# Weight-sum steps moved ahead of an output projection, and the third and fifth activation forms reordered in an MLP's down stages

## The chip, the cores and the metric

The kernel runs on one core of one Trainium2 chip. The metric is the device time of one execution in microseconds, lower is better. The kernel before took 833.65 us (median of 3 runs, 831.7 to 833.7).

## The reference

One encoder layer on 512 tokens of width 1024, in float32: a token mixer (two recurrent head groups behind one input projection, then an output projection), a cross attention on 256 memory tokens, and an MLP of width 4096.

```python
x = x + token_mixer(rmsnorm(x, norm_mix[l]), w_in[l], ...)
x = x + cross_attention(rmsnorm(x, norm_xattn[l]), rmsnorm(mem, norm_mem[l]), w_xq[l], w_xkv[l], w_xo[l])
x = x + squared_relu_mlp(rmsnorm(x, norm_mlp[l]), w_up[l], w_down[l])
return rmsnorm(x, norm_final)

def squared_relu_mlp(xn, w_up, w_down):
    return jnp.square(jax.nn.relu(xn @ w_up)) @ w_down
```

## The kernel before

Every float32 operand is split into a high and a low float32r half (`split_out`, L347: ScalarE writes the high half, VectorE subtracts and writes the low half). A product then is three matmuls: high by high, high by low, low by high. Two splits of a weight tile of 128x1024 feed 12 or 24 matmuls.

From the output projection of the cross attention on, products go by blocks of 2x2 with seven products, P1 to P7, in place of eight. Each product multiplies a **form** of the activations (a block, or a sum of blocks) by a form of the weights. Each of them comes in two halves, 0 and 1, so a stage has 14 jobs; "(P5, 1)" is product P5 with half 1, and in the code's order strings "5b" is the same. The MLP has eight stages: 0, 2, 4 and 6 multiply by `w_up` (function `up`, L1547), 1, 3, 5 and 7 by `w_down` (function `by_blocks`, L1296). The output projection is `by_blocks` with stage -1; the text calls it the output projection, and the odd MLP stages the down stages.

**Weight sums.** The sums of weight blocks for the MLP are made in HBM while the earlier parts of the kernel run. `make_forms` (L309) lists the steps: a copy of a block or of an earlier sum, issued on SyncE's queue (L305 and L321, tile `form_P`), or a transfer that adds a block onto the sum, issued on GpSimd's queue (L305, `form_P<-in_wpk`). `allow(n)` (L250) hands out credit: a copy costs 1, an addition 2. It is called once for each weight tile of the projections (`weights`, L289) and, in the output projection, once for each job with `allow(2)` (L1320). An addition is ordered after the newest weight split on VectorE (`last_made`). SyncE's queue also carries the loads of the weight tiles (tile `st`, L269 and L305), three buffers deep. The sums of the output projection itself are made in SBUF by additions on GpSimd's queue (`add_block`, L1185, tiles `gate` and `as`): after P7's weights are split, another block is added onto the same tile `gate` for P6, and after P6's once more for P4.

**Orders.** TensorE's order is that in which the code is written. VectorE, ScalarE, GpSimd and SyncE are ordered by a scheduler, with `tc.high_priority()` lifting what it encloses; `behind(a, b)` puts instruction a behind b on its engine.

**Forms of the MLP's activations.** An `up` stage makes the forms for the down stage after it: `first(g)` makes P5's, `second` P6's, `by_p3` P3's, `by_p7` P7's, and an unnamed block under `if p in ("P3", "P6")` makes P2's. Some of them are put off into the down stage by the table `turn`, each ahead of a given job. A down stage adds its products onto the residual, tiles `vv`, by `add_to` (L1522, eviction L1525).

Of the kernel before, what the change touches and what calls it, by code (L numbers as in the profile page):

```python
# [80 lines left out]
def trunk(ctx: ExitStack, tc: tile.TileContext, x, mem, wpk, vec, cst, lmask, rmask, rows, out):  # L81
# [201 lines left out]
    def weights(key):  # L283
        i = SIDX[key]
        with (tc.high_priority() if i > 2 else ExitStack()):
            for n in range(i, i + 3):
                split(n)
            load(i + 3)
        allow(0 if i < 6 else 1 if key[1] == "kv" else 2)  # L289
        return hl_tiles[i]  # L290

    mforms = {}
# [930 lines left out]
        MORDER += [seq("1a 5a 1b 6a 2a 3a 7a 5b 6b 4a 2b 7b 3b 4b" if q else "1a 1b 2a 2b 5a 5b 6a 6b 7a 7b 4a 3a 4b 3b"),  # L1223
                   two(*("P1", "P5", "P6", "P2", "P7", "P3", "P4") if q < 3 else ("P1", "P5", "P2", "P6", "P3", "P7", "P4"))]
    MJ = [(st, p, g) for st in range(8) for p, g in MORDER[st]]
    mst, mhl, msum = {}, {}, []

    def mload(n):
        if n < len(MJ) and n not in mst:
# [27 lines left out]
    def msplit(n):  # L1257
        if n >= len(MJ):
            return
        if n not in mhl:  # L1260
            for w in [w for w in due if w[0] <= n]:
                due.remove(w)
                w[1](*w[2:])
            st, p, g = MJ[n]
            mload(n)
            hi, lo = T("wh", 1024, 3, F32R), T("wl", 1024, 3, F32R)
            made = split_out(hi, lo, mst[n])
            last_made[0] = made[1]
            if n == 1:
                q_made[0] = made  # L1270
            mhl[n] = (hi, lo)
            if st % 2 and p == "P6":
                due.append((n + 1, sum_add, st, "P4", g))
            if st % 2 and p in ("P5", "P4") and st < 7:
                q = {"P5": "P5", "P4": "P6"}[p]
                due.append((n + 3, sum_base, st + 2, q, g))
                due.append((n + 7, sum_add, st + 2, q, g))
        return mhl[n]
# [17 lines left out]
    def by_blocks(st, sta, banks, done, ready=None, after=None):  # L1296

        mlp = st >= 0
        user = {"P1": 0, "P2": 1, "P5": 2, "P6": 0, "P3": 2, "P7": 0 if mlp else 3, "P4": 0}
        opens = {"P1", "P2", "P5"} if mlp else {"P1", "P2", "P5", "P7"}  # L1300
        jobs = MORDER[st] if mlp else JOBS
        held = {}

        def product(p, g, u, w, first, end):
            for k in range(2):
                ah, al = [t[:, u * P:u * P + P] for t in sta[2 * g + k][p]]
                bh, bl = [t[:, k * 512:k * 512 + 512] for t in w]
                new = first and k == 0 and p in opens
                fl = dict(skip_group_check=True)
                ps = held[user[p]][u]  # L1310
                pe.matmul(ps, lhsT=ah, rhs=bh, start=new, stop=False, **fl)  # L1311
                pe.matmul(ps, lhsT=ah, rhs=bl, start=False, stop=False, **fl)  # L1312
                pe.matmul(ps, lhsT=al, rhs=bh, start=False, stop=end and k == 1, **fl)  # L1313
            if after is not None:
                after()

        def ahead(n):
            if mlp:
                return mahead(len(JOBS) * st + n)
            allow(2)  # L1320
            with tc.high_priority():
                for m in range(n, n + 3):
                    job(m)
                i = max(hl_tiles)
                for m in range(i + 1, i + 4):
                    load(m)
                for m in range(n + 3 - len(JOBS), n + 7 - len(JOBS)):
                    if m >= 0:
                        mload(m)
            return job(n)  # L1330

        def finished(p, u):
            for t0, c, sign in INTO[mlp][p]:
                done(t0 + u, c, held[user[p]][u], sign, (p, t0, c) in LAST[mlp])

        n = 0
        while n < len(jobs):
            p, g = jobs[n]
            if ready is not None:
                ready(p, g)  # L1340
            if user[p] not in held:
                held[user[p]] = banks[user[p]]()
            if p == "P4":
                ws = [ahead(n), ahead(n + 1)]
                for u in range(2):
                    for g in range(2):
                        product(p, g, u, ws[g], False, g == 1)
                    finished(p, u)
                n += 2
                continue  # L1350
            w = ahead(n)
            for u in range(2):
                product(p, g, u, w, g == 0, g == 1)
                if g == 1:
                    finished(p, u)
            n += 1
# [165 lines left out]
    def add_to(t, c, ps, sign, fin=False):  # L1522
        z = xr[t, c]
        with tc.high_priority():
            added = v.tensor_tensor(out=z, in0=z, in1=ps, op=ALU.add if sign > 0 else ALU.subtract)  # L1525
        if not fin:
            return
        squared = stats(st3, t, c)
# [18 lines left out]
    def up(st):  # L1547
# [4 lines left out]
        def square(t, src):  # L1552
            sc.activation(t, src, AF.Relu)
            sc.activation(t, t, AF.Square)

        def form(p, g, src, buf):
            t = buf(F32R)
            split_out(t[:, 0:512], t[:, 512:1024], src)
            forms[p, g] = t

        def first(g):
            v.tensor_tensor(out=y[3, g], in0=y[2, g], in1=y[3, g], op=ALU.subtract)
            form("P5", g, y[3, g], A4)

        def second(g):
            v.tensor_tensor(out=y[3, g], in0=y[3, g], in1=y[0, g], op=ALU.subtract)
# [8 lines left out]
            form("P7", g, y[0, g], A4)  # L1575

        yt = lambda dt: YT1(dt)
        done = set()
        for n, (p, g) in enumerate(MORDER[st]):
            hi, lo = mahead(len(JOBS) * st + n)  # L1580
            if p == "P1":
# [30 lines left out]
            elif p == "P6":  # L1612
                y[1, g] = rrow[:, (1 - g) * 512:(1 - g) * 512 + 512]
                with tc.high_priority():
                    sc.activation(y[1, g], ps, AF.Copy)
            if p in ("P3", "P6") and {("P3", g), ("P6", g)} <= set(MORDER[st][:n + 1]):
                z = y[1, g]
                v.tensor_tensor(out=z, in0=C[g], in1=z, op=ALU.subtract)
                square(z, z)
                form("P2", g, z, G4)  # L1620
                done.add(("P2", g))
                if ("P4", 0) in done and g == 0:
                    by_p3(0)
            if p == "P7":
                with tc.high_priority():
                    v.tensor_tensor(out=y[3, g], in0=y[3, g], in1=ps, op=ALU.subtract)
# [2 lines left out]
            elif p == "P4":  # L1629
                y[2, g] = T2()[:, 0:512]  # L1630
                with tc.high_priority():
                    square(y[2, g], ps)
                    first(g)
                done.add(("P4", g))
                if g == 0:
                    second(g)
                    by_p7(g)
                    if ("P2", 0) in done:
                        by_p3(g)
        sta = [{} for _ in range(4)]  # L1640

        def hand(g):
# [3 lines left out]
                        sta[2 * g + k][p] = t[:, k * 256:k * 256 + 256], t[:, 512 + k * 256:768 + k * 256]  # L1646

        def ready(p, g):
            for at, fn in turn:
                if (p, g) == at:  # L1650
                    with (tc.high_priority() if fn is second else ExitStack()):
                        fn(1)
                    hand(1)

        turn = ((("P1", 1), second), (("P6", 0), by_p7), (("P2", 0), by_p3))
        if st == 6:
            turn = ((("P1", 1), second), (("P2", 0), by_p3), (("P6", 0), by_p7))
        hand(0)
        hand(1)
        return sta, ready  # L1660
# [97 lines left out]
```

## Time and profile before

| | us |
|---|---|
| median of 3 runs | 833.65 |
| profiled execution, its own time | 833.5 |
| its span, first to last instruction | 831.7 |
| around the span | 1.8 |

The span runs from the mixer's input projection (0 to about 300) over the cross attention (to 447), its output projection (447 to 499) and the MLP's eight stages (499 to the end). In a row of the timeline the columns are start, duration, engine, line, operation, output and input tiles, and in brackets the idle time before it with what ended it. PE is TensorE's matmuls, DVE VectorE, ACT ScalarE, POOL GpSimd. A matmul's duration overlaps the next one, so TensorE's pace is read from the distance of starts. A row of the waits has the waiting engine and line, whom it waited for, the total, the number of times and the longest.

### The profile page before, as it was taken

The numbers are of one execution on the slowest core, as the hardware profiler recorded it, in microseconds if no ns is written. First come the engines' busy times: TensorE is split into PE (matmuls) and PEld (weight loads), VectorE is DVE, ScalarE is ACT, GpSimd is POOL, SyncE is SP. The second block draws the span as 40 slices with busy tenths as digits, with TensorE's granted clock in tenths as the row PEclk, the third lists the DMA queues.
The fourth block names the chain that finished last, engine by engine and source line by source line (L and its number), as shares of the span: only waits on it lengthen the run. The fifth ranks groups of instructions, "written<-read, shape, count | busy, mean of one in ns | idle before, by whom it ended". The sixth has DMA issues, their size and how long they took to land.

```text
span 831.7 us, 14078 instructions
## 1 busy us (share of the span) xinstructions
PE 808.2 (97%) x5438; PEld 696.1 (84%) x5438; DVE 619.1 (74%) x1033; ACT 485.7 (58%) x854; POOL 95.4 (11%) x130
## 2 busy tenths in 40 slices
PE   9999999999999999999999989989999999999995
PEld 6787878877889988887888869978998899789984
DVE  6568885699479898546568859997479658875995
ACT  5247464545577585345455658863586458546854
POOL 2000111201121110211122201010001000100001
PEclk9999999999999999999999999999999999999998
DMA  7367677765795787895689985686866796768552
GB/s 275 117 244 258 149 165 174 206 219 135 182 281 133 185 238 261 249 243 134 148 256 196 237 192 179 203 206 197 261 196 152 227 279 190 171 207 268 178 152 102
DMA packets 56597, 167.26 MB, mean 201 GB/s; under 512 B 5393, under 2 KB 5521, under 8 KB 56530
## 3 DMA queue, kind: packets, MB, share of 16 engines
q1 hardware_dynamic: 41200, 126.04, 44.2%
q0 software_dynamic: 15040, 39.85, 26.4%
q8 instruction: 43, 0.70, 0.3%
q10 hardware_dynamic: 290, 0.47, 0.2%
q14 instruction: 24, 0.20, 0.1%
HBM read 164.24 MB, written 48.23 MB: 255 GB/s over the span
## 4 chain that ended last, share of the span: by engine, by line
PE 77%; DVE 11%; DMA 5%; issue 3%; ACT 2%; POOL 1%; POOLq 0%; SPq 0%; DVEq 0%; ACTq 0%
PE mm L351 11%; PE mm L353 11%; PE mm L352 11%; PE sm L1313 4%; PE sm L1596 4%; PE sm L1311 4%; PE sm L1597 4%; PE sm L1312 4%; PE sm L1595 4%; DVE wl L348 3%; PE mm L1596 3%; PE mm L1597 3%; PE mm L1595 3%; DMA form_P<-form_P 2%; DMA gate<-in_wpk 2%
## 5 line engine op out<-in xcount | busy, mean ns | idle before, releaser
L348 DVE TENSOR_TENSOR wl<-st,wh 128x1024 fp32r<-128x1024 f32 x165 | 201.5, 1223 | 103.2 <-ACT wh L348 102.2
L348 ACT ACTIVATE wh<-st 128x1024 fp32r<-128x1024 f32 x165 | 174.1, 1057 | 167.0 <-PE mm L352 43.9
L351 PE MATMUL mm<-xT,wh 128*128 128x512 f32 x288 | 115.5, 402 | 0.0
L353 PE MATMUL mm<-xT,wl 128*128 128x512 f32 x288 | 113.1, 393 | 0.1
L352 PE MATMUL mm<-xT,wh 128*128 128x512 f32 x288 | 112.8, 392 | 0.3 <-DVE xT L1066 0.3
L305 POOL DMA_DIRECT2D form_P<-in_wpk x44 | 44.8, 1028 | 294.2 <-DVE wl L348 228.9
L1311 PE MATMUL sm<-wh,a 128*128 128x512 f32 x180 | 70.8, 394 | 2.4 <-ACT a L348 2.2
L1313 PE MATMUL sm<-wh,a 128*128 128x512 f32 x180 | 71.3, 396 | 1.6 <-DVE a L348 1.5
L1312 PE MATMUL sm<-wl,a 128*128 128x512 f32 x180 | 70.7, 393 | 0.0
L353 PEld LDWEIGHTS mm<-xT,wl 128*128 128x128 f32 x288 | 54.1, 188 | 11.8 <-DVE wl L348 0.3
L352 PEld LDWEIGHTS mm<-xT,wh 128*128 128x128 f32 x288 | 54.2, 188 | 10.9 <-DVE xT L1066 0.9
L351 PEld LDWEIGHTS mm<-xT,wh 128*128 128x128 f32 x288 | 54.2, 188 | 10.8 <-ACT wh L348 0.3
L305 POOL DMA_DIRECT2D as<-in_wpk x20 | 17.5, 911 | 277.5 <-DVE wl L348 171.9
L1313 PEld LDWEIGHTS sm<-wh,a 128*128 128x128 f32 x180 | 34.2, 190 | 10.4 <-DVE a L348 3.4
L1311 PEld LDWEIGHTS sm<-wh,a 128*128 128x128 f32 x180 | 34.2, 190 | 10.2 <-ACT a L348 2.6
L1312 PEld LDWEIGHTS sm<-wl,a 128*128 128x128 f32 x180 | 34.1, 189 | 7.2
L1596 PE MATMUL sm<-yT,wh 128*128 128x256 f32 x128 | 36.3, 284 | 0.7 <-DVE yT L348 0.7
L348 ACT ACTIVATE wh<-as 128x1024 fp32r<-128x1024 f32 x24 | 25.4, 1057 | 19.8 <-PE sm L1313 12.0
L1596 PE MATMUL mm<-xT,wh 128*128 128x256 f32 x128 | 36.3, 284 | 0.2 <-DVE xT L348 0.2
L1596 PE MATMUL sm<-xT,wh 128*128 128x256 f32 x128 | 36.3, 284 | 0.2 <-DVE xT L348 0.2
L1595 PE MATMUL sm<-xT,wh 128*128 128x256 f32 x128 | 36.4, 284 | 0.0
L1595 PE MATMUL mm<-xT,wh 128*128 128x256 f32 x128 | 36.3, 284 | 0.0
(388 smaller groups left out, 2127.8 us busy)
## 6 DMA issues: line engine op xcount, KB each, us to landing
st<-in_wpk SPq DMA_DIRECT2D x123, 512.0 KB, 4.2
form_P<-in_wpk POOLq DMA_DIRECT2D x44, 512.0 KB, 8.3
st<-form_P SPq DMA_DIRECT2D x42, 512.0 KB, 4.4
form_P<-in_wpk SPq DMA_DIRECT2D x26, 512.0 KB, 6.3
as<-in_wpk POOLq DMA_DIRECT2D x24, 512.0 KB, 7.6
form_P<-form_P SPq DMA_DIRECT2D x18, 512.0 KB, 8.6
gate<-in_wpk POOLq DMA_DIRECT2D x8, 512.0 KB, 7.9
as<-form_P SPq DMA_DIRECT2D x8, 512.0 KB, 5.8
```

What stands on the lines that cost most here:

```text
L305: return eng.dma_start(out=dst, in_=mblock(st, g, *b), max_dma_last_dim=4096, **kw)
L348: return sc.activation(dst_hi, src, AF.Copy), v.tensor_tensor(out=dst_lo, in0=src, in1=dst_hi.bitcast(F32), op=ALU.subtract)
L351: pe.matmul(ps, lhsT=ah, rhs=bh, start=first, stop=False)
L352: pe.matmul(ps, lhsT=ah, rhs=bl, start=False, stop=False)
L353: pe.matmul(ps, lhsT=al, rhs=bh, start=False, stop=last)
L1311: pe.matmul(ps, lhsT=ah, rhs=bh, start=new, stop=False, **fl)
L1312: pe.matmul(ps, lhsT=ah, rhs=bl, start=False, stop=False, **fl)
L1313: pe.matmul(ps, lhsT=al, rhs=bh, start=False, stop=end and k == 1, **fl)
L1595: pe.matmul(o, lhsT=hi[:, z], rhs=xh[:, m], start=new, stop=False, **fl)
L1596: pe.matmul(o, lhsT=hi[:, z], rhs=xl[:, m], start=False, stop=False, **fl)
L1597: pe.matmul(o, lhsT=lo[:, z], rhs=xh[:, m], start=False, stop=kt == 3, **fl)
```

## The change

It has three parts. First, the output projection's `allow(2)` is gone, and each weight tile of the input projection (index 6 to 36) hands out 2.5 credits in place of 2; tiles of the key and value projection keep 1, all others 2. Second, the third form of half 0, `by_p3(0)`, always goes into the down stage, ahead of (P5, 1); and the second form of half 1, now `by_p5(1)`, is made after P4's square in stages 2, 4 and 6. Third, two orders are added: the weight split for (P5, 0) of a down stage stands behind the split of the activation form (P5, 1) on both engines, and every eviction of a down stage stands behind that form's low half on VectorE.

```diff
-        allow(0 if i < 6 else 1 if key[1] == "kv" else 2)
+        allow(0 if i < 6 else 1 if key[1] == "kv" else 2.5 if i < 45 else 2)
...
+            if st % 2 and (p, g) == ("P5", 0):
+                for a, b in zip(made, early["P5", 1]):
+                    behind(a, b)
...
         def ahead(n):
             if mlp:
                 return mahead(len(JOBS) * st + n)
-            allow(2)
...
             added = v.tensor_tensor(out=z, in0=z, in1=ps, op=ALU.add if sign > 0 else ALU.subtract)
+        behind(added, early["P5", 1][1])
...
-            split_out(t[:, 0:512], t[:, 512:1024], src)
+            early[p, g] = split_out(t[:, 0:512], t[:, 512:1024], src)
...
+        def by_p5(g):
+            z = y[1, g]
+            v.tensor_tensor(out=z, in0=C[g], in1=z, op=ALU.subtract)
+            square(z, z)
+            form("P2", g, z, G4)
...
-            if p in ("P3", "P6") and {("P3", g), ("P6", g)} <= set(MORDER[st][:n + 1]):
-                z = y[1, g]
-                v.tensor_tensor(out=z, in0=C[g], in1=z, op=ALU.subtract)
-                square(z, z)
-                form("P2", g, z, G4)
-                done.add(("P2", g))
-                if ("P4", 0) in done and g == 0:
-                    by_p3(0)
+            if p in ("P3", "P6") and {("P3", g), ("P6", g)} <= set(MORDER[st][:n + 1]) and (st == 0 or g == 0):
+                by_p5(g)
...
                     second(g)
                     by_p7(g)
-                    if ("P2", 0) in done:
-                        by_p3(g)
+                elif st:
+                    by_p5(g)
...
-        turn = ((("P1", 1), second), (("P6", 0), by_p7), (("P2", 0), by_p3))
+        turn = ((("P1", 1), second, 1), (("P5", 1), by_p3, 0), (("P6", 0), by_p7, 1), (("P2", 0), by_p3, 1))
         if st == 6:
-            turn = ((("P1", 1), second), (("P2", 0), by_p3), (("P6", 0), by_p7))
+            turn = ((("P1", 1), second, 1), (("P5", 1), by_p3, 0), (("P2", 0), by_p3, 1), (("P6", 0), by_p7, 1))
```

TensorE's order is the same in both kernels, and so are ScalarE's and VectorE's up to the end of stage 0. Line numbers of the changed kernel are higher: an eviction is L1527, `first` L1565, `by_p5` L1570, `second` L1575, `by_p3` L1579, `by_p7` L1583.

The first place is GpSimd's queue in the output projection. Before, the additions onto the MLP's sums (`form_P`) stand between and behind the additions onto the projection's own sums (`gate`); the first two rows are the additions for P6, the second pair of `gate` those for P4.

```order
L1187 DMA gate_4301<-in_wpk 128x1024
L1187 DMA gate_4302<-in_wpk 128x1024
L305 DMA form_P_1_3379<-in_wpk 256x1x512
L305 DMA form_P_1_3391<-in_wpk 256x1x512
L305 DMA form_P_0_3376<-in_wpk 256x1x512
L305 DMA form_P_0_3388<-in_wpk 256x1x512
L1187 DMA gate_4301<-in_wpk 128x1024
L1187 DMA gate_4302<-in_wpk 128x1024
L305 DMA form_P_1_3380<-in_wpk 256x1x512
L305 DMA form_P_1_3392<-in_wpk 256x1x512
```

After, nothing stands between the four, and three additions onto MLP sums remain, behind the two small powers of the norm.

```order
L1187 DMA gate_4311<-in_wpk 128x1024
L1187 DMA gate_4312<-in_wpk 128x1024
L1187 DMA gate_4311<-in_wpk 128x1024
L1187 DMA gate_4312<-in_wpk 128x1024
L1448 TENSOR_TENSOR tiny_5047<-tiny_5044,misc 128x2
L1448 TENSOR_TENSOR tiny_5132<-tiny_5129,misc 128x2
L305 DMA form_P_0_2624<-in_wpk 256x1x512
L305 DMA form_P_1_2616<-in_wpk 256x1x512
L305 DMA form_P_1_2628<-in_wpk 256x1x512
```

Six additions, and the copies between them on SyncE's queue, have moved ahead of the projection.

The second place is ScalarE at the end of stage 0 and the start of stage 1. Before, a_853 is the high half of the activation form (P5, 1), a_849 that of (P3, 0), wh_5670 and wh_5692 are the weights of (P5, 0) and (P5, 1), wh_5714 and wh_5734 those of P6.

```order
L348 ACTIVATE wh_5670<-st_5518 128x1024
L348 ACTIVATE a_844_5556<-as_5137 128x512
L348 ACTIVATE wh_5692<-st_5563 128x1024
L1553 ACTIVATE rg_4656<-rg_4656 128x512
L1554 ACTIVATE rg_4656<-rg_4656 128x512
L348 ACTIVATE wh_5714<-as_5138 128x1024
L348 ACTIVATE gate_5665<-rg_4656 128x512
L348 ACTIVATE wh_5734<-as_5138 128x1024
L348 ACTIVATE a_849_5596<-rg_4656 128x512
L348 ACTIVATE a_853_5631<-t_823_5378 128x512
```

After, a_852 is (P5, 1), a_861 is (P6, 1), and wh_5666 and wh_5688 are the weights of P5.

```order
L348 ACTIVATE gate_5592<-rg_4667 128x512
L348 ACTIVATE a_844_5556<-as_5134 128x512
L348 ACTIVATE a_852_5627<-t_823_5378 128x512
L348 ACTIVATE wh_5666<-st_5518 128x1024
L348 ACTIVATE wh_5688<-st_5563 128x1024
L1556 ACTIVATE rg_4667<-rg_4667 128x512
L348 ACTIVATE a_861_5685<-t_823_5378 128x512
```

The form (P5, 1) has moved from behind eight instructions to ahead of P5's own weights, which it now pushes back.

The third place is VectorE at the same point. Before, the low half of the weights of (P5, 0), wl_5671, is the third row, and the first eviction of stage 1 the seventh.

```order
L1562 TENSOR_TENSOR t_823_5378<-t_852_5627,t_823_5378 128x512
L1574 TENSOR_TENSOR as_5137<-as_5137,t_841_5544 128x512
L348 TENSOR_TENSOR wl_5671<-st_5518,wh_5670 128x1024
L348 TENSOR_TENSOR a_844_5556<-as_5137,a_844_5556 128x512
L348 TENSOR_TENSOR gate_5592<-rg_4656,gate_5592 128x512
L1618 TENSOR_TENSOR rg_4656<-mm_5353,rg_4656 128x512
L1525 TENSOR_TENSOR vv_3639<-vv_3639,sm_5668 128x512
```

After, from the same two instructions on:

```order
L1565 TENSOR_TENSOR t_823_5378<-t_851_5623,t_823_5378 128x512
L1583 TENSOR_TENSOR as_5134<-as_5134,t_841_5544 128x512
L348 TENSOR_TENSOR gate_5592<-rg_4667,gate_5592 128x512
L1570 TENSOR_TENSOR rg_4667<-mm_5353,rg_4667 128x512
L348 TENSOR_TENSOR a_852_5627<-t_823_5378,a_852_5627 128x512
L348 TENSOR_TENSOR a_844_5556<-as_5134,a_844_5556 128x512
L1575 TENSOR_TENSOR t_823_5378<-t_823_5378,as_5135 128x512
L1527 TENSOR_TENSOR vv_3650<-vv_3650,sm_5664 128x512
L348 TENSOR_TENSOR wl_5667<-st_5518,wh_5666 128x1024
```

The low half of (P5, 1) is now ahead of the first eviction, and the low half of (P5, 0)'s weights, wl_5667, has moved from the third row to the ninth, behind that eviction.

More of the change, by code (lines that the diff above doesn't have):

```diff
@@ L1225, in trunk @@
     MJ = [(st, p, g) for st in range(8) for p, g in MORDER[st]]
-    mst, mhl, msum = {}, {}, []
+    mst, mhl, msum, early = {}, {}, [], {}
     def mload(n):
@@ L1577, in up @@
         yt = lambda dt: YT1(dt)
-        done = set()
         for n, (p, g) in enumerate(MORDER[st]):
@@ L1633, in up @@
                     first(g)
-                done.add(("P4", g))
                 if g == 0:
@@ L1648, in ready @@
         def ready(p, g):
-            for at, fn in turn:
+            for at, fn, h in turn:
                 if (p, g) == at:
                     with (tc.high_priority() if fn is second else ExitStack()):
-                        fn(1)
-                    hand(1)
-        turn = ((("P1", 1), second), (("P6", 0), by_p7), (("P2", 0), by_p3))
+                        fn(h)
+                    hand(h)
+        turn = ((("P1", 1), second, 1), (("P5", 1), by_p3, 0), (("P6", 0), by_p7, 1), (("P2", 0), by_p3, 1))
         if st == 6:
-            turn = ((("P1", 1), second), (("P2", 0), by_p3), (("P6", 0), by_p7))
+            turn = ((("P1", 1), second, 1), (("P5", 1), by_p3, 0), (("P2", 0), by_p3, 1), (("P6", 0), by_p7, 1))
         hand(0)
```

## The prediction

> **What bounds the kernel now.** I read the page's first part, then TensorE's waits, then the timeline about the longest of them.
>
> ```profile
> span 831.7 us, 14078 instructions
> PE 808.2 (97%) x5438; PEld 696.1 (84%) x5438; DVE 619.1 (74%) x1033; ACT 485.7 (58%) x854; POOL 95.4 (11%) x130
> ```
>
> TensorE is busy for 97% of the span, and its instructions and their order stay the same. So the change can only win by closing holes in front of matmuls, or lose by opening some. TensorE's waits say where the holes are:
>
> ```profile
> PE sm L1423 <- DVE vv L1397: 2.6, 1, 2.6
> PE sm L1311 <- ACT a L348: 2.2, 1, 2.2
> PE mm L1312 <- DVE wl L348: 0.8, 1, 0.8
> ...
> PE mm L352 <- DVE wl L348: 0.2, 1, 0.2
> ```
>
> The first and third lie in the output projection, the second at the start of stage 1; the last is in the input projection, the only wait for a split weight there. Recorded waits are not the whole loss, so I count by windows: from the projection's last norm to the MLP's first matmul, and from the first matmul of P5 to that of P2 in stages 1, 3 and 5. The columns are window, length, busy times of PE, PEld, DVE, ACT and POOL with counts, granted clock, DMA share, GB/s.
>
> ```profile
> 485.09:499.24 14.15, 10.26 (x47) 7.87 (x46) 8.77 (x14) 11.35 (x25) 0.71 (x1) 0.88 0.75 175
> 547.62:562.79 15.17, 12.98 (x49) 9.91 (x48) 13.24 (x18) 7.77 (x11) 2.69 (x3) 0.89 0.90 221
> 630.33:641.94 11.61, 11.22 (x50) 8.93 (x48) 11.40 (x16) 7.11 (x10) 2.62 (x3) 1.00 0.58 104
> 709.48:721.84 12.36, 11.21 (x50) 8.93 (x48) 12.15 (x17) 7.38 (x10) 2.62 (x3) 1.00 0.59 120
> ```
>
> To know what these should last, I need the pace of TensorE. Its rows in the output projection:
>
> ```profile
> 483.72 0.39 PE L1311 MATMUL sm<-wh,a 128*128 128x512 f32 x1
> ...
> 485.09 1.03 PE L1423 MATMUL sm<-cs,vv 128*128 128x128 f32 x8
> 486.52 0.49 PE L1311 MATMUL mm<-wh,yT 128*128 128x512 f32 x1 [0.40 <-ACT wh L348]
> 487.78 0.50 PE L1312 MATMUL mm<-wl,yT 128*128 128x512 f32 x1 [0.76 <-DVE wl L348]
> 488.11 0.39 PE L1313 MATMUL mm<-wh,yT 128*128 128x512 f32 x1
> 488.34 0.40 PE L1311 MATMUL mm<-wh,yT 128*128 128x512 f32 x1
> ...
> 491.81 2.35 PE L1423 MATMUL sm<-cs,vv 128*128 128x128 f32 x8 [2.60 <-DVE vv L1397]
> ...
> 498.89 0.60 PE L1423 MATMUL sm<-cs,vv 128*128 128x128 f32 x4
> 499.24 0.36 PE L1595 MATMUL sm<-xT,wh 128*128 128x256 f32 x1
> ```
>
> Six matmuls start between 483.72 and 485.09: 1.37 / 6 = 0.228 us each. A transpose takes between 0.35 / 4 = 0.09 (498.89 to 499.24) and 1.03 / 8 = 0.13; I take 0.11.
>
> The first window holds 24 matmuls and 22 transposes: 24 x 0.228 + 22 x 0.11 = 7.9 us. It lasts 14.15, so **6.2 us are lost**. The other windows hold 48 matmuls, 48 x 0.228 = 10.96: **4.2, 0.65 and 1.4 us are lost** in stages 1, 3 and 5.
>
> **The change, part 1: the output projection.** What is late there is P4's weights:
>
> ```profile
> 485.41 1.06 ACT L348 ACTIVATE wh<-gate 128x1024 fp32r<-128x1024 f32 x1 [7.17 <-DMA gate<-in_wpk]
> 493.03 3.01 ACT L1430 ACTIVATE a<-sm,vc 128x256 f32<-128x256 f32 x8
> ```
>
> ScalarE idled 7.17 us for the addition onto `gate`. GpSimd's queue shows why, and the DMA issues (median time from issue to landing in the last column) show the additions for P6, issued in 447.5 to 452, and those for P4:
>
> ```profile
> 473.62 1.03 POOL L305 DMA_DIRECT2D form_P<-in_wpk  x1 [6.76 <-DMA form_P<-form_P]
> 474.18 2.32 POOL L1187 DMA_DIRECT2D gate<-in_wpk  x2
> ```
>
> ```profile
> gate<-in_wpk POOLq DMA_DIRECT2D x2, 512.0 KB, 5.8
> ```
>
> ```profile
> gate<-in_wpk POOLq DMA_DIRECT2D x2, 512.0 KB, 12.6
> ```
>
> P4's additions stood behind a weight-sum addition that waited 6.76 us for its copy, and then took 12.6 us beside it instead of 5.8. The order shows that nothing stands between them now. Even issued no sooner than 474.18 they would land at 474.18 + 5.8 = 480.0, and the splits (1.06 on ScalarE, 1.22 on VectorE) end by 482.3. TensorE is ready for them at 486.12 (486.52 less the wait of 0.40), so the weights may land as late as 486.12 - 2.28 = 483.8. That removes the waits of 0.40, 0.76 and 2.60 and the slow matmuls behind the last. What is late next is the norm: the eight copies on ScalarE (3.01 us) lie beneath TensorE's waits today and end 3.2 us ahead of the MLP's first matmul; closer to its start they will leave a part of a wait. I leave 0.6 to it, an estimate between nothing and the 3.01. **Gain 5.6**; ends 0.6 (the additions issue 474.18 - 473.62 earlier and still take 12.6) and 6.2.
>
> **Part 2: steps moved into the input projection.** Six additions and the copies between them, 2 or 1 credits each, now run before the cross attention, between loads of weights on SyncE's queue and on GpSimd's. Every projection tile issues half a step more or less, so no queue gets a new kind of neighbour, but each of them gets fuller. The trace has two waits for split weights beside such steps, 0.2 (input projection) and 0.8 (output projection), quoted above. **Cost 0.5**, their middle; the lower end is 0, since the 0.2 of now is all that 2 credits a tile bring; the upper end is the rival R3 below.
>
> **Part 3: the down stages.** The start of stage 1 now, on TensorE and ScalarE:
>
> ```profile
> 552.69 0.50 PE L1311 MATMUL sm<-wh,a 128*128 128x512 f32 x1 [2.19 <-ACT a L348]
> ...
> 554.11 0.63 PE L1311 MATMUL sm<-wh,a 128*128 128x512 f32 x1
> 554.53 0.63 PE L1312 MATMUL sm<-wl,a 128*128 128x512 f32 x1
> ...
> 556.63 0.39 PE L1311 MATMUL sm<-wh,a 128*128 128x512 f32 x1
> ```
>
> ```profile
> 543.80 0.64 ACT L348 ACTIVATE a<-as 128x512 fp32r<-128x512 f32 x1 [0.16 <-DVE as L1574]
> ...
> 550.54 1.06 ACT L348 ACTIVATE wh<-as 128x1024 fp32r<-128x1024 f32 x1 [1.04 <-PE sm L1313]
> 551.51 0.61 ACT L348 ACTIVATE a<-rg 128x512 fp32r<-128x512 f32 x1
> 552.02 0.61 ACT L348 ACTIVATE a<-t 128x512 fp32r<-128x512 f32 x1
> ```
>
> The high half of (P5, 1) is split at 552.02, behind a weight split that waits for TensorE to give back a buffer (550.54) and behind the form (P3, 0), which is not needed for long. TensorE waits 2.19 us; then nine matmuls take 556.63 - 552.69 = 3.94 in place of 9 x 0.228 = 2.05, with the pace at 0.42 (554.11 to 554.53). So 2.2 + 1.9 = 4.1 of the 4.2 hang on this one split.
>
> The Trainium skill, "TensorE: Matmul & The Clock Gate", section "What's actually happening", says that the clock halves only after at least one idle window of about 3.4 us. The trace has the slow pace behind an idle time of 2.19 already, so I count the slow stretch as part of the wait; by the rule alone it would come from elsewhere and stay, which is rival R4.
>
> In the changed order (P5, 1) comes right behind (P7, 0): 543.80 + 0.51 (the distance from 551.51 to 552.02) = 544.31, ending at 544.95, long before it is needed. But P5's own weights now stand behind it. On VectorE:
>
> ```profile
> 542.48 0.68 DVE L1562 TENSOR_TENSOR t<-t,t 128x512 f32<-128x512 f32 x1
> 543.08 0.68 DVE L1574 TENSOR_TENSOR as<-as,t 128x512 f32<-128x512 f32 x1
> 543.68 1.22 DVE L348 TENSOR_TENSOR wl<-st,wh 128x1024 fp32r<-128x1024 f32 x1
> ```
>
> Such rows start 0.60 apart. The low half of (P5, 1) can start at 544.95; then come the low half of (P7, 0), `second` and the first eviction: the weights' low half starts at 544.95 + 4 x 0.60 = 547.35 and ends 1.22 later, at 548.57, where it now starts at 543.68. TensorE wants it for the second matmul of P5, 547.62 + 0.23 = 547.85. That is a **new wait of 0.7 us**. Short waits slow nothing: behind the one of 0.76 matmuls stand 0.23 apart again (488.11, 488.34). Gain in stage 1: 4.2 - 0.7 = 3.5.
>
> In stages 3 and 5 the same instructions move by about as much. There, 0.65 + 1.4 = 2.05 can go at most. If each gets the new wait of 0.7 in full, it is 2.05 - 1.4 = 0.65. I take the middle, 1.3. At stage 7 no loss is counted and no gain. The order behind the split for every eviction costs nothing by itself: the split is ahead of the first eviction in the order shown, and the second form of half 1 that now waits for P4's square feeds P2, four jobs of 12 matmuls later (4 x 2.7 us). **Gain of the part 4.8**; ends 0.65 and 6.25.
>
> **Sum.** The profiled execution took 833.5 (span 831.7 and 1.8 around it), 0.15 below the median of 833.65, which is as good as the same. 833.5 - 5.6 - 4.8 + 0.5 = **823.6 us**.
>
> **The rivals.** R1: P5's weights come later than I reckon, by another low split (1.22) in each of three stages, since two edges push them back and ScalarE's half, wh, must also be in. 3 x 1.2 = 3.6 is eaten: 827.2. For it speaks that the margin is already negative; against it, that the weights are loaded early enough to be split at 543.68 now. Chance 0.10.
>
> R2: P4's additions take 12.6 us for another reason than the neighbour, for instance the weight loads on SyncE's queue, which stay beside them. The gain of part 1 is 0.6 in place of 5.6: 828.6. It decides if they land later than 483.8. For it: what the neighbour costs is inferred from two groups of two; against it, the 7.17 us of ScalarE and the 6.76 of GpSimd line up. Chance 0.12.
>
> R3, the slower side: fuller queues in the input projection. A copy on SyncE's queue that waits for an addition holds the weight loads behind it:
>
> ```profile
> SPq L321 <- DMA form_P<-in_wpk: 16.3, 4, 7.6
> ```
>
> ```profile
> st<-in_wpk SPq DMA_DIRECT2D x12, 512.0 KB, 4.0
> ```
>
> ```profile
> st<-in_wpk SPq DMA_DIRECT2D x4, 512.0 KB, 12.1
> ```
>
> The longest such wait is 7.6 us; the next tile of weights lasts 24 x 0.228 = 5.5, so 2.1 would show on TensorE. The loads (second fence, 140 to 235) land in 4.0 us, against 12.1 beside the additions of the projection (third, 447 to 486), so neighbours can triple a load. In the changed order, about ten times a copy that depends on an addition stands ahead of a weight load. With the gains of 10.4 kept, 833.5 - 10.4 = 823.1 and 2.1 for each place: at five places 833.6, no change; from seven, 837.8, slower, which is the rival's time. Against it: the four recorded waits brought 0.2 in the input projection. Chance 0.07, of it 0.04 for slower and 0.03 for no change. The Trainium skill, "DMA: Bandwidth & Descriptors", section "Queues, rings and completion order", has the engines take turns between queues packet by packet; a load beside one busy queue would then at most double, which speaks against R3. The 12.1 against 4.0 does not bear that out, so its chance stays.
>
> R4: the slow stretches stay though the waits go. They are 1.9 in stage 1 and 2.35 - 1.03 = 1.3 in the projection's transposes: 823.6 + 3.2 = 826.8. Chance 0.02.
>
> **How the numbers follow.** The forecast has 0.69. The range: all that is lost today gone and part 2 free gives 833.5 - 6.2 - 6.25 = 821.05, less 1.0, half the spread of the runs of before (831.7 to 833.7): 820.0. Above, it takes in R1, R4 and R2 with the same 1.0: 828.6 + 1.0 = 829.6. About 0.1 lies outside by R3, and some by my sizes. A change under 0.3%, 2.5 us, can't be told from none, so "same" is 831.15 to 836.15. Faster is the forecast with R1, R2 and R4, 0.93; same 0.03; slower 0.04.
>
> **What would show it.** Right: P4's additions take about 6 us and land before 483.8 less the shift of the program; no wait at the projection's L1423; its window of 46 instructions near 8.5 us; stage 1's near 11.7, with a wait of about 0.7 <- DVE wl at P5's second matmul and no matmuls 0.42 apart. Wrong: loads of `st` in the input projection of well over 4.0 us with TensorE waiting for wh or wl (R3), additions of 12 us on `gate` (R2), waits of 2 us at P5 of each down stage (R1).

## The result and the profile after

The changed kernel took 828.17 us (median of 5 runs, 825.8 to 829.4) against 833.65 (5 runs, 831.7 to 834.6): a ratio of 0.9934, 95% interval 0.9911 to 0.9958. It is faster by 5.5 us, where 10.05 had been forecast. Its profiled execution took 825.79, the fastest of the five, so the traces differ by 7.7 us and the medians by 5.5. One execution of e5_noedge below, the profiled one, ran at a granted clock of 0.85 throughout and took 880.91 us, and it is left out of that experiment's time.

TensorE runs the same 5438 matmuls in the same order in both, so both traces can be cut at the same matmuls:

| stretch, by matmuls of the trace before | before | after | forecast of the change | measured |
|---|---|---|---|---|
| up to the projection's last norm | 485.09 | 485.32 | +0.5 | +0.2 |
| the projection's last norm to the MLP | 14.15 | 7.85 | -5.6 with the next row | -6.3 |
| MLP start to 520.06 | 20.82 | 21.23 | | +0.4 |
| **520.06 to 525.96, stage 0** | 5.90 | 8.06 | 0 | **+2.2** |
| P5 to P2 of stage 1 | 15.17 | 11.84 | -3.5 | -3.3 |
| **570.04 to 580.02, later in stage 1** | 9.98 | 10.92 | 0 | **+0.9** |
| P5 to P2 of stages 3 and 5 | 23.97 | 22.55 | -1.3 | -1.4 |

Every term of the sum came out within 0.3 us. What is missing is two losses in rows to which the sum had given nothing. The windows of those two rows before the change, in the columns of the prediction:

```profile
520.06:525.96 5.90, 5.18 (x44) 4.97 (x43) 5.18 (x6) 4.68 (x6) 0.00 (x0) 1.00 0.90 311
570.04:580.02 9.98, 9.98 (x46) 8.26 (x44) 6.69 (x8) 3.89 (x4) 0.00 (x0) 1.00 0.64 199
```

The windows of the changed kernel:

```profile
485.32:493.17 7.85, 7.85 (x48) 6.69 (x46) 5.38 (x10) 7.45 (x19) 0.71 (x1) 1.00 0.21 68
514.40:522.46 8.06, 5.44 (x43) 5.04 (x42) 5.17 (x6) 4.58 (x6) 0.00 (x0) 1.00 1.06 315
544.13:555.97 11.84, 11.17 (x49) 8.93 (x48) 11.64 (x15) 6.92 (x10) 2.67 (x3) 1.00 0.76 190
563.23:574.15 10.92, 10.28 (x46) 8.18 (x45) 8.25 (x10) 4.85 (x5) 0.88 (x1) 1.00 0.89 278
624.46:635.39 10.93, 10.93 (x49) 9.01 (x48) 10.82 (x14) 6.14 (x8) 2.65 (x3) 1.00 0.69 143
702.93:714.55 11.62, 11.18 (x49) 8.93 (x48) 11.55 (x15) 6.94 (x10) 2.66 (x3) 1.00 0.61 128
```

In the first, TensorE is busy all the time: the projection's end has no hole left. In the second it is busy 5.44 of 8.06 us, and the DMA share is 1.06 in place of 0.90. In the fourth it is 0.89 in place of 0.64. No window has a clock below 1.00, where the windows of before had 0.88 at the projection's end and 0.89 at the start of stage 1. TensorE's waits:

```profile
PE sm L1315 <- DVE wl L348: 1.8, 3, 0.7
PE sm L1603 <- ACT yT L348: 1.7, 1, 1.7
...
PE sm L1604 <- DVE yT L348: 0.9, 1, 0.9
```

The waits of 2.6 and 2.2 are gone, and the forecast wait of 0.7 for P5's weights is there (0.67 in stage 1 and 0.44 in stage 5; the third of that row, 0.64, lies in the later part of stage 1). But a wait of 1.7 and 0.9 for `yT`, the activations of stage 0, is new. ScalarE and then TensorE at that place:

```profile
517.61 1.06 ACT L348 ACTIVATE wh<-st 128x1024 fp32r<-128x1024 f32 x1 [2.56 <-DMA st<-form_P]
518.58 0.58 ACT L1623 ACTIVATE rg<-sm 128x512 f32<-128x512 f32 x1
519.05 1.05 ACT L348 ACTIVATE yT<-a 128x1024 fp32r<-128x1024 f32 x1
```

```profile
518.12 0.28 PE L1605 MATMUL sm<-yT,wl 128*128 128x256 f32 x1
520.15 0.38 PE L1603 MATMUL sm<-yT,wh 128*128 128x256 f32 x1 [1.75 <-ACT yT L348]
521.41 0.38 PE L1604 MATMUL sm<-yT,wh 128*128 128x256 f32 x1 [0.88 <-DVE yT L348]
```

ScalarE stands 2.56 us before a weight split whose load (`st<-form_P`) is late, and the split of `yT`, which needs no load, stands behind it in the queue. Before, ScalarE had no wait for a load between 505 and 526. GpSimd issues three additions onto weight sums in this stage (first fence). The load issued between 508 and 512 takes 7.4 us beside them (second fence), where the same load of before took 3.4 (third fence, issued between 514 and 518 of before):

```profile
501.85 1.09 POOL L305 DMA_DIRECT2D form_P<-in_wpk  x1
506.96 1.04 POOL L305 DMA_DIRECT2D form_P<-in_wpk  x1 [4.03 <-DVE wl L348]
513.31 1.03 POOL L305 DMA_DIRECT2D form_P<-in_wpk  x1 [5.30 <-DVE wl L348]
```

```profile
form_P<-in_wpk POOLq DMA_DIRECT2D x1, 512.0 KB, 10.2
st<-form_P SPq DMA_DIRECT2D x1, 512.0 KB, 7.4
```

```profile
st<-form_P SPq DMA_DIRECT2D x1, 512.0 KB, 3.4
```

These are the additions that the credits of 2.5 leave over. Before, six additions ran in the projection, between 456 and 480. Only three of them have moved ahead of it, not six as the text on the change says; the other three have moved behind it, into stage 0. **Theory A** says that they cost the 2.2 us; its rival **B** is that the norm's chain is only closer to the MLP's start. **Theory C** says that the 0.9 us in stage 1 are also late loads; its rival puts them down to the earlier end of the projection. **Theory D** is on the third part: the put-off form does the work, and the two orders on P5's weights only cost the 0.7; its rival is that the orders are needed.

### The profile page after: what moved, and what is told of

Same layout as the page of the kernel before. It is cut to its first block, busy times and chain, and to the rows that moved or that the text cites. A ratio compares the mean times of both kernels' runs of the same rounds, so it can differ in the third digit from the quotient of the medians.

```text
span 824.0 us, 14080 instructions
## 1 busy us (share of the span) xinstructions
PE 803.1 (97%) x5438; PEld 693.2 (84%) x5438; DVE 618.6 (75%) x1033; ACT 486.1 (59%) x854; POOL 95.4 (12%) x130
## 4 chain that ended last, share of the span: by engine, by line
PE 72%; DVE 11%; DMA 6%; issue 5%; ACT 5%; POOL 1%; POOLq 0%; ACTq 0%; DVEq 0%
PE mm L351 11%; PE mm L352 11%; PE mm L353 11%; PE sm L1315 5%; PE sm L1316 4%; PE sm L1314 4%; DVE wl L348 4%; PE sm L1604 2%; DMA st<-in_wpk 2%; PE sm L1605 2%; PE sm L1603 2%; ACT wh L348 2%; DMA st<-form_P 2%; PE mm L1604 1%; PE mm L1605 1%
## 5 line engine op out<-in xcount | busy, mean ns | idle before, releaser
L1314 PE MATMUL sm<-wh,a 128*128 128x512 f32 x180 | 70.3, 391 | 0.1
L1316 PE MATMUL sm<-wh,a 128*128 128x512 f32 x180 | 70.1, 390 | 0.0
L1603 PE MATMUL sm<-yT,wh 128*128 128x256 f32 x128 | 36.3, 284 | 1.7 <-ACT yT L348 1.7
L1604 PE MATMUL sm<-yT,wh 128*128 128x256 f32 x128 | 36.3, 284 | 0.9 <-DVE yT L348 0.9
## 6 DMA issues: line engine op xcount, KB each, us to landing
form_P<-form_P SPq DMA_DIRECT2D x18, 512.0 KB, 10.2
```

The lines of the kernel that those rows point to most:

```text
L1603: pe.matmul(o, lhsT=hi[:, z], rhs=xh[:, m], start=new, stop=False, **fl)
L1604: pe.matmul(o, lhsT=hi[:, z], rhs=xl[:, m], start=False, stop=False, **fl)
```

## The experiments

All are compared with the kernel before on the same chip; windows are of one profiled execution each.

**e1_c275: no additions left for stage 0.** From the changed kernel:

```diff
-        allow(0 if i < 6 else 1 if key[1] == "kv" else 2.5 if i < 45 else 2)
+        allow(0 if i < 6 else 1 if key[1] == "kv" else 2.75 if i < 45 else 2)
```

> The changed kernel with 2.75 credits for a tile of the input projection in place of 2.5, so that no addition onto a weight sum is left for MLP stage 0 (three are left in the changed kernel). Theory A (the three additions make the loads of stage 0 land late, 7.4 us in place of 3.4, a split on ScalarE waits for one of them, and the activations' split stands behind it): the 2.15 us that the changed kernel loses near 520 us go, the stretch that lasts 8.06 there is back at 5.9, and the time is about 2.1 us below the changed kernel's, near 826 at its median. Theory B (the norm's chain is simply closer to the MLP's start because the projection ends 6 us sooner): the stretch stays at 8.1 and the time stays at 828. If the input projection does not bear more steps, its part up to 485 us grows by 1 us or more.

Measured: 824.41 us, ratio 0.9879 (0.9854 to 0.9905). Its stretch in stage 0, and the landing of the load issued between 508 and 512:

```profile
514.28:520.18 5.90, 5.17 (x44) 4.97 (x42) 5.18 (x6) 4.69 (x6) 0.00 (x0) 1.00 0.88 312
```

```profile
st<-form_P SPq DMA_DIRECT2D x1, 512.0 KB, 3.3
```

The stretch is back at 5.90 and the load at 3.3 us: theory A holds, B falls. The part up to the projection's last norm is unchanged (485.2 against 485.3), so the input projection bears the steps. The interval of its ratio lies wholly below that of the change. The two profiled executions took the same, 825.8: what this one gained in stage 0 it lost in stage 7, by a wait of 1.56 for an eviction and one of 0.6 for weights. e10_tail is on the first.

**e4_c2: more additions left.** The same line with 2 in place of 2.5, so that eight are left.

> The changed kernel with 2 credits for a tile of the input projection, as before the change: eight additions and their copies are left for MLP stage 0. Theory A: the loss in stage 0 grows with the additions, from 2.15 us with three to 4 us or more with eight, and the time is 830 or more. Theory B: the loss in stage 0 stays 2.15 and the time stays at 828. Either way the output projection should stay at about 7.9 us from the last norm's transposes to the MLP, since nothing stands between its own additions.

Measured: 832.38 us, ratio 0.9978 (0.9960 to 0.9996). The projection's window is 7.85. Four of the eight additions run in stage 0 (issued at 508 to 529) and four in stage 1 (550 to 569), and the loss is spread in the same way. In the stretch near 520 it is 2.3 us, hardly more than with three additions, where 4 or more had been expected. The next stretch lasts 22.7 in place of 21.7, the start of stage 1 12.6 in place of 11.84, and the later part of stage 1 14.36 in place of 10.92:

```profile
515.57:523.78 8.21, 5.90 (x44) 5.50 (x42) 5.63 (x6) 4.57 (x6) 1.03 (x1) 0.94 1.07 327
566.32:580.68 14.36, 12.16 (x46) 9.32 (x44) 9.11 (x11) 4.83 (x5) 1.97 (x2) 0.88 1.08 277
```

With none, three and eight additions left over, the kernel takes 824.4, 828.2 and 832.4.

**e2_credits: the credits alone**, on the kernel before.

```diff
-        allow(0 if i < 6 else 1 if key[1] == "kv" else 2)
+        allow(0 if i < 6 else 1 if key[1] == "kv" else 2.5 if i < 45 else 2)
...
-            allow(2)
```

> The kernel before with the credits of the change alone: no steps in the output projection, 2.5 for a tile of the input projection; forms and orders of the down stages as before. Theory A: the output projection's window falls from 14.15 to about 7.9 us, 2.15 are lost again in stage 0, the start of stage 1 stays at 15.2; together 3.8 less than before, 829.8. Rival (the additions for P4 are slow for another reason than their neighbour): the window stays near 13.5 and the time near 833.

Measured: 828.97 us, ratio 0.9942 (0.9921 to 0.9962). The projection's window is 7.85, the stretch in stage 0 8.84, the start of stage 1 15.35: as theory A has it, with 0.8 more lost in stage 0 than in the changed kernel, at a clock of 0.90. P4's additions land in 5.5 and 5.6 us here, and in 12.3 and 15.0 in e3_down, which has the weight-sum steps in the projection. So they were slow because of those neighbours.

**e3_down: the down stages alone**, the changed kernel with the credits of before.

> The down stages' part of the change alone: forms and orders as in the changed kernel, credits as before it. The start of stage 1 falls from 15.2 to 11.8 us, stages 3, 5 and 7 gain 0.7, 0.7 and 0.4 and the output projection stays at 14.2. Theory C (the later part of stage 1 gives back 0.9 us since its loads are now closer together and share the queues with its additions): the stretch behind its P2 grows from 10.0 to 10.9 here too, and the time is 833.65 - 5.1 + 0.9 = 829.4. Rival (what is given back there comes from the earlier end of the projection): the stretch stays at 10.0 and the time is 828.5.

Measured: 829.41 us, ratio 0.9947 (0.9927 to 0.9966). The start of stage 1 is 11.83 and the stretch behind P2 11.00, against 9.98 before: what stage 1 gives back comes from its own faster start. (The projection's window was 16.12 in this execution, 2.0 longer than before.)

The next six have 2.75 credits, as e1_c275.

**e7_later: two copies and two additions later in stage 1.** The edit moves them by six jobs, not by the three of the text below, and so among the first loads for stage 2. The copies are issued at 559.6 and 562.0, where e1_c275 issues them at 545.0 and 551.2, and the additions at 566.7 and 570.0 in place of 552.4 and 562.5.

```diff
-                due.append((n + 3, sum_base, st + 2, q, g))
-                due.append((n + 7, sum_add, st + 2, q, g))
+                w = 6 if (st, p) == (1, "P5") else 0
+                due.append((n + 3 + w, sum_base, st + 2, q, g))
+                due.append((n + 7 + w, sum_add, st + 2, q, g))
```

> With 2.75 credits as in e1_c275, and the two copies that begin stage 3's sums in SBUF (tile as, on SyncE's queue in stage 1) three jobs later and so in stage 2's first loads, their additions too. Theory C (the loads of stage 1 are late since they share the queues with these copies and with additions): weight loads that take 7.6 to 8.8 us there take 5 to 6, and the stretch behind P2 of stage 1 falls from 10.96 to about 10.0; 1 us less, about 823.5. Rival (the additions on GpSimd's queue alone, which stay, or the order of the splits): the stretch stays at 10.9.

Measured: 823.88 us, ratio 0.9883 (0.9859 to 0.9908), against 0.9879 of e1_c275: the times don't tell them apart. The stretch does, 9.98 in place of 10.96, with TensorE busy throughout:

```profile
560.91:570.89 9.98, 9.98 (x46) 8.26 (x44) 6.70 (x8) 3.89 (x4) 1.73 (x2) 1.00 0.95 295
```

The loads ahead of it, in the changed kernel (issued 552 to 557), and here (issued 550.7 to 554.5):

```profile
as<-in_wpk POOLq DMA_DIRECT2D x2, 512.0 KB, 9.0
st<-form_P SPq DMA_DIRECT2D x1, 512.0 KB, 7.7
as<-in_wpk SPq DMA_DIRECT2D x1, 512.0 KB, 10.7
st<-in_wpk SPq DMA_DIRECT2D x1, 512.0 KB, 8.7
```

```profile
st<-form_P SPq DMA_DIRECT2D x1, 512.0 KB, 5.1
st<-in_wpk SPq DMA_DIRECT2D x1, 512.0 KB, 4.0
```

Theory C holds, with one thing open: the copies and the additions were moved together, so it is not shown which of them made the loads late. The DMA share does not tell a late load by itself: it is 0.95 here without a loss, and 0.89 in the changed kernel with one. What this execution gained here it lost again at the end of stage 7, by a wait of 1.25 for an eviction; e10_tail is on that.

**e6_nodefer: the orders without the put-off form.** `by_p3(0)` is made in the up stage again, as before the change; all orders stay.

> With 2.75 credits as in e1_c275, all orders of the change kept, but the third form of half 0 made in the up stage as before. Theory D: the form's square and split stand on ScalarE and VectorE ahead of (P5, 1) again, the start of stage 1 grows from 11.84 to 13 or more, since the weights of P5 now have to wait behind it. Rival (the orders alone do it): the start of stage 1 stays at 11.8.

Measured: 840.31 us, ratio 1.0080 (1.0049 to 1.0111), slower than before. TensorE's waits and the three starts of down stages:

```profile
PE sm L1315 <- DVE wl L348: 9.7, 5, 2.3
```

```profile
542.62:557.57 14.95, 12.65 (x49) 10.12 (x50) 13.05 (x17) 7.10 (x9) 2.63 (x3) 0.89 0.71 163
626.16:641.37 15.21, 12.92 (x48) 10.25 (x49) 13.04 (x17) 6.58 (x8) 2.63 (x3) 0.89 0.51 102
709.17:724.34 15.17, 12.88 (x49) 10.26 (x49) 13.05 (x17) 6.59 (x8) 2.62 (x3) 0.89 0.51 102
```

P5's weights now wait for a form that comes late, 2.3 us at the longest, and the clock of each window is 0.89. This is what the prediction's R1 feared of the orders; but where R1 priced it at 1.2 a stage, these starts are 3.1, 4.3 and 3.7 us longer than in e1_c275 (11.84, 10.93 and 11.48), slow pace included. The orders alone are a loss; with the form put off they are cheap.

**e5_noedge: the put-off form without the order on P5's weights** (on ScalarE and VectorE).

```diff
-            if st % 2 and (p, g) == ("P5", 0):
-                for a, b in zip(made, early["P5", 1]):
-                    behind(a, b)
```

> With 2.75 credits as in e1_c275, and without the two orders that put the weights of (P5, 0) of a down stage behind the split of (P5, 1). Theory D (the orders cost the wait of 0.7 us for the low half of the weights, and it is the put-off third form that brings (P5, 1) forward): the waits of 0.7 at the second matmul of P5 go in stages 1 and 5, stage 1's start falls from 11.84 to about 11.1, about 1.4 us in all. Rival: without the orders the scheduler puts (P5, 1) late again, the wait of 2.2 <- ACT a is back and the start of stage 1 lasts 15.2.

Measured: 822.13 us (median of three), ratio 0.9866 (0.9838 to 0.9895), against 0.9879 of e1_c275: the times don't tell them apart. The windows are read from e9_both, which repeats the edit.

**e8_noevict: evictions free**, without `behind(added, early["P5", 1][1])`.

> With 2.75 credits as in e1_c275, and without the order that puts every eviction of a down stage behind the low half of (P5, 1). By my sum this order costs and brings nothing: same time within 0.3%, the start of stage 1 at 11.8. Rival: an eviction then stands ahead of that low half, it starts 0.6 us later and TensorE waits for a, or the weights' low half gets an eviction less ahead of it and the wait of 0.7 becomes shorter.

Measured: 823.66 us, ratio 0.9880 (0.9851 to 0.9909), the start of stage 1 11.86. This order does nothing that can be measured.

**e9_both: the edits of e7_later and e5_noedge together.**

> 2.75 credits, stage 3's sums begun three jobs later (as e7_later), and no orders that put P5's weights behind the split of (P5, 1) (as e5_noedge). Theory D: the waits of 0.7 for P5's weights go, stage 1's start is 11.1 in place of 11.85 and stages 3, 5 and 7 start within 11.1, together 1 to 2 us less than e7_later; the load of the last norm's weights stands behind the last weight load again, so no wait at the end; 821.5 at its median. Rival: (P5, 1) is late in some stage without the orders, with a wait for a, and the time is that of e7_later, 823.9, or more.

Measured: 821.8 us, ratio 0.9849 (0.9824 to 0.9873), the fastest kernel of this study. Starts of stages 1, 3 and 5 and the later part of stage 1:

```profile
541.90:552.78 10.88, 10.88 (x49) 9.01 (x48) 10.85 (x15) 7.26 (x10) 1.76 (x2) 1.00 0.71 145
560.04:570.01 9.97, 9.97 (x45) 8.26 (x44) 7.33 (x9) 3.89 (x4) 1.73 (x2) 1.00 0.90 292
620.32:631.20 10.88, 10.88 (x49) 9.01 (x48) 10.80 (x16) 5.93 (x8) 2.62 (x3) 1.00 0.51 89
698.77:709.65 10.88, 10.88 (x49) 9.01 (x48) 10.80 (x16) 5.92 (x7) 2.62 (x3) 1.00 0.53 98
```

TensorE is busy for the whole of all four, and each start is the 10.96 of the prediction's pace, or a little less. e7_later, which has the orders, takes 11.85 at the start of stage 1. So their wait costs 11.85 - 10.88 = 1.0 us there, and theory D holds. The medians of the two differ by 2.1 us, but their intervals overlap a little. The other half of the change's second part, `by_p5(1)` after P4's square, is in all of these runs; no experiment takes it out, so its share is not shown.

**e10_tail: the last norm's weights behind the last weight load.** On SyncE's queue the change had moved the 512 KB of `rg<-in_rows` ahead of the last `st<-form_P`; e9_both, without the two orders, has it behind again. Here the orders stay, and the load is issued behind.

```diff
-        if f == 3:
-            gfin = RG()
-            nc.sync.dma_start(out=gfin, in_=rows[3:4, :].to_broadcast([P, D]))
...
+            if st == 7 and (p, g) == ("P7", 1):
+                last7.append(RG())
+                behind(nc.sync.dma_start(out=last7[-1], in_=rows[3:4, :].to_broadcast([P, D])), last_load[0])
```

> As e7_later, with all orders of the change, but the load of the last norm's weights (tile rg, 512 KB, from in_rows) stands behind the last weight load of stage 7 on SyncE's queue, as in the kernel before; the change moved it ahead. Theory E (that load, beside the last weight load, makes it land after 6.65 to 6.95 us in place of 5.1 to 5.9, and then TensorE waits 1.2 to 1.6 us in stage 7): the last weight load lands in 5.5 us or less, no wait behind a VectorE eviction in stage 7, the stretch from 801 us of before to its last matmuls is 21.4 to 21.6 in place of 22.6, the time about 1 us below e7_later. Rival: these waits come with another transfer, or vary from run to run for no cause in the queue, and the time stays at 823.9.

Measured: 823.15 us, ratio 0.9869 (0.9840 to 0.9899). The last load, in e7_later and here:

```profile
st<-form_P SPq DMA_DIRECT2D x1, 512.0 KB, 6.7
```

```profile
st<-form_P SPq DMA_DIRECT2D x1, 512.0 KB, 4.7
rg<-in_rows SPq DMA_DIRECT2D x1, 512.0 KB, 5.5
```

It lands 2 us sooner, the eviction's wait is gone, and the last stretch is 21.3 in place of 22.6. The other traces bear out the first half of theory E: the last weight load lands in 5.8 to 6.9 us in seven executions that have the load of `rg` ahead of it (the changed kernel twice, e1_c275, e3_down, e4_c2, e7_later, e8_noevict), and in 4.7 to 5.5 in four that have it behind (before, e2_credits, e9_both, e10_tail). The second half is weaker: waits of over 1 us for an eviction came only at 6.7 and 6.9 (e7_later, e1_c275), and three of the seven had none. Why the load lands at 5.9 in one execution and at 6.9 in another stays open, and the times of e7_later and e10_tail don't differ by more than their intervals.

**e11_again: the changed kernel once more.**

> The changed kernel once more, since its profiled execution (825.8) was the fastest of its five (825.8 to 829.4, median 828.2). Theory F (what differs between executions is how long loads take where the queues are full: stage 0 beside the three additions, and the last weight load of stage 7 beside the load for the last norm): a profiled execution that is 1 to 3 us longer has it in the stretch near 520 (over 8.06) or at the end of stage 7 (over 21.5, up to 22.9). Rival: the longer time is spread over the whole program, or lies in the mixer (its part to 485 us grows by 1 us or more).

Measured: 827.1 us, ratio 0.9922 (0.9899 to 0.9946). The profiled execution took 827.8, 2.0 more than the first. Of that, 1.1 lie in and behind the stretch near 520 (8.40 in place of 8.06, then 22.47 in place of 21.67). Its window, and TensorE behind the second wait for `yT`:

```profile
514.23:522.63 8.40, 6.14 (x43) 5.74 (x42) 5.87 (x6) 4.56 (x6) 0.00 (x0) 0.90 1.06 326
```

```profile
520.87 0.46 PE L1604 MATMUL sm<-yT,wh 128*128 128x256 f32 x1 [0.88 <-DVE yT L348]
521.13 0.42 PE L1605 MATMUL sm<-yT,wl 128*128 128x256 f32 x1
521.35 0.42 PE L1603 MATMUL sm<-yT,wh 128*128 128x256 f32 x1
...
524.51 0.28 PE L1603 MATMUL sm<-yT,wh 128*128 128x256 f32 x1
524.63 0.28 PE L1604 MATMUL sm<-yT,wh 128*128 128x256 f32 x1
```

The waits are no longer than in the first execution (1.4 and 0.88 against 1.75 and 0.88). But here matmuls stand 0.22 apart behind them (521.13 to 521.35) until 524.5, in place of 0.12 (524.51 to 524.63), with a clock of 0.90 in the window; in the first execution they stood 0.12 apart at once. Of the rest, 0.5 is at P5 of stage 3 and about 1 at P5 of stage 7, where TensorE waits 0.83 for the weights' low half, with 0.7 less in stage 5; the tail (21.3) and the part up to 485 us have no share. Theory F names the right place in stage 0, with another cause than longer waits for the loads, and the wrong end of stage 7.

## Why the prediction was right, and where it was not

The time lies inside the range and the way is right, but the 828.17 lies near the 828.6 that the range had taken in for R2, and R2 did not come about: P4's additions landed in 5.3 and 5.7 us, the second with a weight load beside it. What took its place are two losses without a term in the sum. So the forecast of 823.6 was missed by 4.6 us, and that the range holds the time is in part luck.

**The output projection (5.6).** Right in cause and size: 6.3 in the window, of which 0.4 come back at the MLP's start; e2_credits has it without the rest. The slow matmuls went with the waits (the clock of the window is 1.00 in place of 0.88), there and at the start of stage 1, so R4 falls as well.

**The input projection (+0.5, up to R3).** It cost 0.2, and at 2.75 credits no more. R3 did not come about there. Copies on SyncE's queue waited for an addition as often as before, four times (15.5 us in all and 8.8 at the longest, before 16.3 and 7.6), not the ten times of R3. The weight loads issued between 140 and 235 landed in 3.8 us (4.0 before), and TensorE's wait for `wl` stayed at 0.2.

**The start of stage 1 (3.5) and stages 3 and 5 (1.3).** Right: 3.3 and 1.4. The new wait was counted at 0.7 and measured at 0.67; with what follows it costs 1.0, as e9_both shows. What the working had wrong is who does it: it treated the put-off form and the two orders as one thing. e6_nodefer, e5_noedge and e9_both show that the form is the gain and that the orders on P5's weights are a price that need not be paid. One slip stands in the ends of part 3: the lower end of 0.65 leaves out the 3.5 of stage 1. The range did not use it.

**What failed** is part 2 of the sum: it has six additions run before the cross attention, where three did. The text on the change shows the other three behind the norm's two small powers; the sum has no term for them. In the projection they had stood before and behind P4's additions, and TensorE had no wait there for a weight load. In stage 0 they stand beside loads that TensorE needs at once, and cost 2.2 us. R3 had the mechanism (loads of 4.0 that take 12.1 beside additions), and looked for it in the wrong place.

**The second gap** is in part 3, which took what stage 1 loses at its start for what the stage would gain. Stage 1 lost 0.9 of its 3.3 again, since its loads and the sums for stage 3 had used the hole. The question "what is late next" was asked of the engines, not of the queues.

**Stage 7.** "At stage 7 no loss is counted." There is none in the first execution of the changed kernel. In others the orders' wait came there too (0.6 in e1_c275, 0.83 in e11_again), and in the two in which the last weight load took 6.7 and 6.9 us, behind the load of `rg` that had moved past it, TensorE waited 1.25 and 1.56 at the end.

The median stands 2.4 us above the profiled execution. e11_again puts about half of such a difference on the slow pace that follows the new waits in stage 0 in some executions; so the three additions cost 2.2 us in one execution and 3.3 in another. The other half stays open.

## What to carry to other kernels

A budget of background transfers that is taken from one place must be followed to where its remainder lands: three additions left over decided whether this change gave 5.5 us (7.0 when it was measured again) or the 9.3 of e1_c275. When a hole in front of the busiest engine closes, look at which transfers had been living in it. And an order that holds one step behind another is worth only as much as the other step is early: make it early first, then ask whether the order is still needed.

## What the runs showed of the hardware

A 512 KB load that lands in 3.3 to 3.4 us (e1_c275 and before) took 7.4 in the changed kernel, with an addition from GpSimd's queue in flight beside it. A copy on the load's own queue took 7.7 beside the same addition, and 4.1 in e1_c275. The addition itself took 10.2, where those for P4 in the changed kernel's projection, issued at 471 and 474 us with little beside them, took 5.5. The Trainium skill, "DMA: Bandwidth & Descriptors", section "Queues, rings and completion order", says that the engines take turns between queues packet by packet, by which a load beside one busy queue would take about twice as long, an estimate from that rule. The 7.4 against 3.4 is near it, though the copy stood ahead of the load as well; the 12.1 against 4.0 of the prediction is not.

TensorE's slow pace (matmuls of 512 columns 0.43 apart in place of 0.23) came behind every wait of 2.19 us or more from the projection on: 2.60 and 2.19 before, 2.19 in e2_credits, 2.41 in e3_down, and 2.29 or 2.30 four times in e6_nodefer. It began at once or up to 1.5 us later. It never came behind a wait that stood alone and was shorter (1.56 in e1_c275, 1.41 in e4_c2, 1.25 in e7_later, 0.7 in many). Behind a pair of waits, mostly that for `yT`, it came in e11_again (1.4 and 0.88), e2_credits (1.72 and 0.88) and e4_c2 (1.44 and 0.88, and 1.44 and 0.76 for weights in stage 1), and not in the first execution of the changed kernel (1.75 and 0.88). The Trainium skill, "TensorE: Matmul & The Clock Gate", section "What's actually happening", has the clock watched in windows of about 3.4 us that run freely; that such a pair is followed by both agrees with it. Its condition, at least one idle window, does not: none of these waits reached 3.4 us. For a forecast on this kernel, a single hole of 2.2 us or more is to be priced at up to twice its length (2.19 + 1.9 in the kernel before); between 1.6 and 2.2 no run here shows a hole that stands alone.
